# Route to the experts: residual's affine part moved to VectorE, tokens gathered as normalised values and modulated as columns

## The chip, the cores and the metric

One core of one Trainium2 chip runs the whole program. The metric is the device time of one execution in microseconds, lower is better. Three executions of the kernel before took 2433.91, 2436.0 and 2442.73 us; the median is 2436.0 us. The names used below: PE is TensorE, DVE is VectorE, ACT is ScalarE, POOL is GpSimd, SP is SyncE, whose queue issues the weight loads.

## The reference, cut to what matters

The program is two transformer blocks of two layers each on 256 tokens (and 256 context tokens) of width 1024, in float32. Only the two layers of the first block are touched. Each of them ends its mixer with a layer norm, a modulation, a router and a mixture of 32 experts:

```python
x = layer_norm(ALPHA * x + g1x * yx, ln1_g[l], ln1_b[l])     # layer 0 also for ctx, with its own g1c
ux = x * (1.0 + s2x) + sh2x                                  # layer 0: uc = ctx * (1.0 + s2c) + sh2c
y = hier_moe(tok, ...)                                       # top 2 of 32 experts, weights 1024x512, 1024x512, 512x1024
x = layer_norm(ALPHA * x + g2x * y, ln2_g[l], ln2_b[l])
```

With z the normalised row (before gain and bias), the experts' input is z * (g(1+s2)) + (b(1+s2) + sh2), and the residual is ALPHA * (z*g + b). In layer 0 there are 512 tokens (four tiles of 128: tiles 0 and 1 are x, tiles 2 and 3 are ctx, with different s2 and sh2); in layer 1 there are 256 (two tiles, one pair of s2 and sh2).

## The kernel before, in words

`out_ln` multiplies the mixer's output by its weight matrix, adds the residual, normalises each row and computes the router's logits. In layer 0 it does this in two passes, first for tiles 2 and 3, then for tiles 0 and 1. `normalise` leaves z in the residual's tile (`M.x`, called mx in the trace; in layer 1 it is xres). `modulate` then makes the experts' input: in layer 0 a product and a sum with two 128x1024 tiles A and B that hold gain and bias broadcast to all partitions (on POOL or DVE by the list `MODL`), and a split of the result into two float32r halves uh and ul (`split_T`: uh on ACT, ul on POOL), written with the columns permuted. In layer 1 only the split is done there; gain and bias enter later as columns. `route` ranks the tokens (a chain of small DVE instructions, L593 to L639, with three PE products between them). `modulate` for tiles 0 and 1 is queued behind the chain's mark (L574), and after it POOL multiplies each residual tile by ALPHA*g and adds ALPHA*b (L578 and L579, 128x1024 each).

`moe` runs the experts in units of two: 16 units in layer 0, 15 in layer 1, each with 12 weight tiles of 1 MB. The weights come on SP's queue into a ring of 11 tiles, in the order of the code; a tile is loaded again when PE has read it. `gather` collects the 128 token slots of a unit: DVE builds a one-hot matrix Pm (L735, L736: two instructions per token tile), PE multiplies uh and ul by it (L748), and ACT copies the result from PSUM to xT (L753; in layer 1 with scale and bias as columns, L759). Unit 0 is gathered alone, later units in pairs. `unit` multiplies xT by the gate and up weights (gu, L825), forms hh (L829 on ACT, L830 on DVE), transposes it (hT), multiplies by the down weights (ey, L851) and returns eight (four in layer 1) scatters: PE spreads the result back over the tokens (sc, L871 and L872), DVE scales it (gy, L875), POOL adds it to the residual (L876). From unit 1 on the order on PE is the order of the code; the scatters of the unit before and the gather of the next pair are put between the gu products by the lists `FILL` (the `work` callback). Before unit 0 the planner of the framework orders the instructions by readiness and by place in the code; `issue_after(m)` only keeps an instruction behind m on m's own engine. Between unit 0 and unit 1 stands a conditional block (`rest`, L967) that all engines pass. PSUM has four buffers for gathers, scatters and transposes together (`psB`).

Of the kernel before, what the change touches and what calls it, by code (L numbers as in the profile page):

```python
# [21 lines left out]
D = 1024  # L22
# [20 lines left out]
MODL = ((0, 1, 1, 0), (0, 0))  # L43
BOTH = (1, 0, 1)


# [86 lines left out]
class Kernel:  # L133
# [349 lines left out]
    def out_ln(self, M, W, lhs, L, ntt, xsrc):  # L483
        nc, I, ada = self.nc, self.I, self.ada[L]
        self.rate = RATE_O
        with self.pool("po") as p:
            g1 = [self.bcast(p, ada.dram[i, 2048:3072], D, f"g1_{i}") for i in range(ntt // 2)]
            lg = self.bcast(p, I["ln1_g"][L], D, "lng")
            lb = self.bcast(p, I["ln1_b"][L], D, "lnb")
            ns = ntt // 2  # L490
            WA, red = self.wa, self.red
            A, B = [], []
            for i in range(ns if L == 0 else 0):
                sh = self.bcast(p, ada.dram[i, 3072:4096], D, f"B{i}")
                sc = self.bcast(p, ada.dram[i, 4096:5120], D, f"A{i}")
                tmp = p.tile([128, D], F32, name="AB", tag="u", bufs=2)
                nc.gpsimd.tensor_scalar(sc, sc, 1.0, 1.0, op0=OP.mult, op1=OP.add)
                nc.gpsimd.tensor_mul(tmp, sc, lb)
                nc.gpsimd.tensor_add(sh, sh, tmp)
                nc.gpsimd.tensor_mul(sc, sc, lg)  # L500
                A.append(sc)
                B.append(sh)
            for v in (lg, lb):
                nc.gpsimd.tensor_scalar(v, v, ALPHA, 0.0, op0=OP.mult, op1=OP.add)
            if L == 0:
                for t in range(ntt):
                    nc.sync.dma_start(M.x[t], xsrc[t])
                xsrc = M.x
            else:
                M.cols = self.ucols  # L510
            z = M.x
            st = p.tile([128, ntt, 2, 6], F32, name="ln_st")
            norm = {}
            MOD = [(nc.gpsimd, nc.vector)[k] for k in MODL[0]]
            MOD1 = [(nc.gpsimd, nc.vector)[k] for k in MODL[1]]
# [6 lines left out]
            def modulate(t, eng):  # L522
                v8 = lambda a: a.rearrange("t (p j) -> t p j", j=8)
                jt = lambda a: a.rearrange("t j p -> t p j")
                if L == 0:
                    u = p.tile([128, 8, 128], F32, name="u", tag="u", bufs=2)
                    eng.tensor_mul(jt(u), v8(z[t]), v8(A[t // 2]))
                    eng.tensor_add(jt(u), jt(u), v8(B[t // 2]))
                    return self.split_T(M.uh[t], M.ul[t], u, nc.gpsimd)
                else:  # L530
                    return self.split_T(jt(M.uh[t]), jt(M.ul[t]), v8(z[t]), eng)

            def logits(c, tts):

                for t in tts:
                    pt = self.psB("zT")
                    for k in range(4):
# [12 lines left out]
                    nc.vector.bn_aggr(mv, st[:, t])  # L550
                    r = self.rsqrt(mv[:, 1:2], 1e-5, [128, 1], bufs=4)
                    norm[t] = (mv, r)
                    nc.vector.scalar_tensor_tensor(g, red[:, t // 2, 0], mv[:, 0:1], g, op0=OP.mult, op1=OP.add)
                    nc.vector.scalar_tensor_tensor(g, g, r, red[:, t // 2, 1], op0=OP.mult, op1=OP.add)

            for tts in (((2, 3), (0, 1)) if ntt > 2 else ((0, 1),)):
                def ev(c, tt, ps):
                    sl = slice(c * 512, c * 512 + 512)
                    gy = self.sb.tile([128, 512], F32, name="gy", tag="s512")
                    nc.vector.tensor_mul(gy, ps, g1[tt // 2][:, sl])  # L560
                    nc.vector.scalar_tensor_tensor(z[tt][:, sl], xsrc[tt][:, sl], ALPHA, gy,
                                                   op0=OP.mult, op1=OP.add)
                    nc.vector.bn_stats(st[:, tt, c], z[tt][:, sl])
                    if tt == tts[-1]:
                        logits(c, tts)
                self.lin_D(W, lhs, tts, ev, (0, 4), L == 1 and BOTH[0])
                for t in tts:
                    normalise(t)
                if tts[0] == 2:
                    for t in tts:  # L570
                        modulate(t, MOD[t])
# [148 lines left out]
    def gather(self, M, base, sl, places=(0,)):  # L720


        nc, n, p = self.nc, M.ntt, M.wp
        V = nc.vector
        stat = not isinstance(base, bass.AP)

# [15 lines left out]
        def part(c):  # L742
            pg = self.psB("xT")
            for a in range(per):
                j = per * c + a
                for t in ts:
                    for k, u in enumerate((M.uh[t], M.ul[t])):
                        nc.tensor.matmul(pg[:, a * w:a * w + w], u[:, j], Pm[:, t, :w],  # L748
                                         start=t == ts[0] and k == 0, stop=t == ts[-1] and k == 1)
            js = slice(per * c, per * c + per)  # L750
            for i in range(m):
                if M.cols is None:
                    xt = nc.scalar.activation(  # L753
                        xT[i][:, js], pg.rearrange("p (j m t) -> p m j t", m=m, t=128)[:, i], AF.Copy)
                    continue
# [6 lines left out]
        return xT, [lambda c=c: part(c) for c in range(2 * m)]  # L762

    def unit(self, M, base, experts, widths, room=2048, xT=None, work=None):

# [95 lines left out]
        yh = p.tile([128, 2, 512], F32R, name="yh", tag="yh", bufs=1)  # L861
        yl = p.tile([128, 2, 512], F32R, name="yl", tag="yl", bufs=1)
# [16 lines left out]
    def moe(self, M):  # L879
# [19 lines left out]
        for tag in ("yh", "yl"):  # L899
            M.wp.tile([128, 2, 512], F32R, name=tag, tag=tag, bufs=1)  # L900
        M.rows = None
        units = UNITS[L]

# [14 lines left out]
        def run(u, add, parts):  # L918
# [1123 lines left out]
```

## Time and profile before

| | before |
|---|---|
| median of three executions | 2436.0 us |
| profiled execution | 2441.86 us |
| its span | 2439.7 us |
| PE busy | 2218.6 us (91%) |
| DVE busy | 1254.7 us (51%) |
| ACT busy | 708.4 us (29%) |
| POOL busy | 537.6 us (22%) |
| mean granted TensorE clock (share of full) | 0.951 |
| HBM traffic | 266 GB/s over the span |
| a 512 KB weight load, from issue to landing | 10.2 us (median) |

The page gives busy time of each engine, the span in 40 slices, the DMA queues, the chain of work that ended last, and the costliest groups of instructions. A busy PE is not PE at its peak. In the timeline each row is a start time, a duration from the first start to the last end, the engine, the line, the operation, and how many instructions were merged; in brackets is how long the engine was idle before and who released it.

### The profile page before, as it was taken

What the parts mean: (1) busy time and instruction counts of PE and PEld (TensorE: products, weight loads), DVE (VectorE), ACT (ScalarE), POOL (GpSimd) and SP (SyncE); (2) the same over time, 40 slices, a digit from 0 to 9 for tenths busy, and PEclk for the clock granted to TensorE, in tenths of its full rate; (3) what the DMA queues carried; (4) which work ended last, traced back from release to release, by engine and by line L of the source; (5) the groups of instructions that cost most, each with busy time, mean ns of one, the idle gap of its engine ahead of it and who ended that gap; (6) DMA issues with size and microseconds to landing.
All of it is one profiled execution on the core that took longest, in us unless ns stands there. A gap on an engine that the chain in (4) does not pass through costs nothing. (4 is left out here: it accounts for less than half of the span.)

```text
span 2439.7 us, 35230 instructions
## 1 busy us (share of the span) xinstructions
PE 2218.6 (91%) x13185; PEld 1395.5 (57%) x13186; DVE 1254.7 (51%) x2724; ACT 708.4 (29%) x1179; POOL 537.6 (22%) x451
## 2 busy tenths in 40 slices
PE   7999995789999998899779999998899999858999
PEld 3786673444444443676633333332655998657997
DVE  3354767444444444757842322223774554666554
ACT  2215242111111111434421111111453543414442
POOL 2121334233333333300130211111201000561000
PEclk9999996699999999899979999999899999979999
DMA  8654365389999999443569999999554555737553
GB/s 301 249 193 156 134 213 223 129 342 408 408 409 409 409 408 373 155 173 132 191 240 384 409 408 408 409 409 380 190 191 172 191 176 186 261 107 274 186 179 120
DMA packets 209272, 652.36 MB, mean 267 GB/s; under 512 B 20668, under 2 KB 33965, under 8 KB 197568
## 3 DMA queue, kind: packets, MB, share of 16 engines
q1 hardware_dynamic: 201680, 632.24, 68.9%
q0 software_dynamic: 7408, 17.73, 2.2%
q8 instruction: 107, 1.75, 0.3%
q14 instruction: 77, 0.63, 0.1%
HBM read 648.65 MB, written 1.25 MB: 266 GB/s over the span
## 5 line engine op out<-in xcount | busy, mean ns | idle before, releaser
L825 PE MATMUL gu<-w,xT 128*32 128x512 f32 (+1 forms) x2880 | 493.0, 605 | 16.2 <-PEq L967 9.9
L201 DVE TENSOR_TENSOR wlo<-w,whi 128x1024 fp32r<-128x1024 f32 (+3 forms) x240 | 298.7, 1246 | 308.6 <-ACT whi L200 308.4
L200 ACT ACTIVATE whi<-w 128x1024 fp32r<-128x1024 f32 (+3 forms) x264 | 274.2, 1041 | 508.4 <-PE A L247 276.8
L825 PEld LDWEIGHTS gu<-w,xT 128*32 128x32 f32 (+1 forms) x2880 | 141.0, 121 | 315.5 <-issue 246.4
L1872 PE MATMUL A<-lhs_hi,wlo 128*128 128x256 f32 x864 | 246.5, 286 | 14.1 <-POOL wlo L201 13.6
L246 PE MATMUL A<-wlo,lhs_hi 128*128 128x512 f32 (+3 forms) x640 | 248.7, 389 | 9.5 <-DVE wlo L201 9.4
L245 PE MATMUL A<-whi,lhs_hi 128*128 128x512 f32 (+3 forms) x640 | 250.6, 396 | 5.9 <-ACT whi L200 2.8
L1870 PE MATMUL A<-lhs_hi,whi 128*128 128x256 f32 x864 | 247.8, 287 | 1.0 <-ACT whi L200 1.0
L1871 PE MATMUL A<-lhs_lo,whi 128*128 128x256 f32 x864 | 247.1, 286 | 0.0
L247 PE MATMUL A<-whi,lhs_lo 128*128 128x512 f32 (+3 forms) x640 | 246.6, 386 | 0.0
L876 POOL TENSOR_TENSOR mx<-mx,gy 128x512 f32<-128x512 f32 x124 | 161.5, 1331 | 355.0 <-DVE gy L875 354.9
L851 PE MATMUL ey<-w,hT 128*32 128x512 f32 (+1 forms) x1440 | 225.8, 595 | 9.5 <-ACT hT L838 9.5
L875 DVE TENSOR_TENSOR gy<-sc,g 128x512 f32<-128x512 f32 x188 | 121.5, 685 | 218.2 <-PE sc L872 215.8
L1872 PEld LDWEIGHTS A<-lhs_hi,wlo 128*128 128x128 f32 x864 | 167.8, 194 | 14.5 <-POOL wlo L201 13.8
L1870 PEld LDWEIGHTS A<-lhs_hi,whi 128*128 128x128 f32 x864 | 167.9, 195 | 7.1 <-issue 5.0
L1871 PEld LDWEIGHTS A<-lhs_lo,whi 128*128 128x128 f32 x864 | 168.0, 194 | 0.2 <-DVE lhs_lo L255 0.2
L876 POOL TENSOR_TENSOR xres<-xres,gy 128x512 f32<-128x512 f32 x58 | 74.3, 1293 | 380.0 <-DVE gy L875 379.1
L245 PEld LDWEIGHTS A<-whi,lhs_hi 128*128 128x128 f32 x640 | 123.1, 194 | 56.3 <-issue 17.7
L851 PEld LDWEIGHTS ey<-w,hT 128*32 128x32 f32 (+1 forms) x1440 | 68.3, 120 | 147.9 <-issue 115.6
L246 PEld LDWEIGHTS A<-wlo,lhs_hi 128*128 128x128 f32 x640 | 123.4, 193 | 39.6 <-DVE wlo L201 13.8
L748 PE MATMUL xT<-Pm,uh 128*128 128x256 f32 (+1 forms) x416 | 111.4, 303 | 29.4 <-DVE Pm L736 29.4
L247 PEld LDWEIGHTS A<-whi,lhs_lo 128*128 128x128 f32 x640 | 123.5, 193 | 24.2 <-issue 4.0
(586 smaller groups left out, 3264.8 us busy)
## 6 DMA issues: line engine op xcount, KB each, us to landing
w<-in_moe_w_gate_dram SPq DMA_DIRECT2D x248, 512.0 KB, 10.2
w<-in_moe_w_up_dram SPq DMA_DIRECT2D x248, 512.0 KB, 10.2
w<-in_moe_w_down_dram SPq DMA_DIRECT2D x248, 512.0 KB, 10.2
w<-in_ada_w_dram SPq DMA_DIRECT2D x88, 1024.0 KB, 6.7
w<-in_ffn_w_dram SPq DMA_DIRECT2D x64, 1024.0 KB, 5.1
w<-in_ab_w_in_dram SPq DMA_DIRECT2D x13, 1024.0 KB, 9.0
w<-in_c_w_qkv_dram SPq DMA_DIRECT2D x12, 1024.0 KB, 5.2
w<-in_ada_w_dram SPq DMA_DIRECT2D x16, 512.0 KB, 9.9
```

What stands on the lines that cost most here:

```text
L200: self.nc.scalar.activation(hv, w, AF.Copy)
L201: (eng or self.nc.vector).tensor_sub(lv, w, hv.bitcast(F32))
L245: nc.tensor.matmul(o, hi[:, kk, ts], wh[:, k], start=at + k == 0, stop=False)
L246: nc.tensor.matmul(o, hi[:, kk, ts], wl[:, k], start=False, stop=False)
L247: nc.tensor.matmul(o, lo[:, kk, ts], wh[:, k], start=False, stop=at + k == nk - 1)
L825: nc.tensor.matmul(pgu[m][a:b], xT[:, j, a:b], w[:, i, k], start=j == 0, stop=j == 7)
L851: nc.tensor.matmul(py[h][a:b], hT[:, j, a:b], w[:, i, k, h * 512:h * 512 + 512], start=j == 0, stop=j == 3)
L875: V.tensor_mul(gy, ps, M.g2[t // 2][:, h * 512:h * 512 + 512])
L876: eng.tensor_add(o, o, gy)
L1870: nc.tensor.matmul(o, wh[:, k, cs], hi[:, kk], start=kk == 0 and c % 2 == 0, stop=False)
L1871: nc.tensor.matmul(o, wh[:, k, cs], lo[:, kk], start=False, stop=False)
L1872: nc.tensor.matmul(o, wl[:, k, cs], hi[:, kk], start=False, stop=kk == 7 and c % 2 == 1)
```

## The change

In layer 0, `out_ln` no longer loads A and B as broadcast tiles. Six vectors are loaded as columns (128 partitions by 8) and combined by five small POOL instructions into scale columns for x and ctx, shift columns for ctx, and the difference of the two shifts. `modulate` becomes `parts`, in both layers only the split of z, with uh on ACT and ul on DVE. POOL's products and sums on the residual go. In `moe` two tiles that later hold the experts' results (yh and yl) first take g and b (loaded broadcast on POOL's queue, scaled by ALPHA on ACT), and `residual` does the products and sums on DVE, queued behind the Pm of units 1 and 2, from the `work` callback of unit 0. In layer 0, `gather` uses `part2`: the slots' share of x tokens is counted by a product of ones with Pm (of_x, plain float32, two products and a copy by ACT), ctx tokens and x tokens are gathered into separate halves of a PSUM buffer (a buffer holds half as many columns), and each 128x128 block is evicted by one ACT instruction and two DVE instructions instead of part of an ACT copy. `begin(1)`, which builds Pm for units 1 and 2, is called before unit 0 is written instead of after.

```diff
@@ out_ln
-            for i in range(ns if L == 0 else 0):
-                sh = self.bcast(p, ada.dram[i, 3072:4096], D, f"B{i}")
-                sc = self.bcast(p, ada.dram[i, 4096:5120], D, f"A{i}")
...
-            for v in (lg, lb):
-                nc.gpsimd.tensor_scalar(v, v, ALPHA, 0.0, op0=OP.mult, op1=OP.add)
+                cols = M.p.tile([128, 6, 8], F32, name="ucols0")
+                for k, v in enumerate((ada.dram[0, 4096:5120], ada.dram[1, 4096:5120], ada.dram[0, 3072:4096],
+                                       ada.dram[1, 3072:4096], I["ln1_g"][L], I["ln1_b"][L])):
+                    nc.gpsimd.dma_start(cols[:, k], v.rearrange("(p j) -> p j", j=8))
...
+            def parts(t):
                 v8 = lambda a: a.rearrange("t (p j) -> t p j", j=8)
                 jt = lambda a: a.rearrange("t j p -> t p j")
-                if L == 0:
-                    u = p.tile([128, 8, 128], F32, name="u", tag="u", bufs=2)
-                    eng.tensor_mul(jt(u), v8(z[t]), v8(A[t // 2]))
-                    eng.tensor_add(jt(u), jt(u), v8(B[t // 2]))
-                    return self.split_T(M.uh[t], M.ul[t], u, nc.gpsimd)
-                else:
-                    return self.split_T(jt(M.uh[t]), jt(M.ul[t]), v8(z[t]), eng)
+                self.split_T(jt(M.uh[t]), jt(M.ul[t]), v8(z[t]))
...
             for t in (0, 1):
                 with self.tc.issue_after(mark):
-                    last = modulate(t, MOD[t] if L == 0 else MOD1[t])
-            with self.tc.issue_after(last):
-                for t in norm:
-                    nc.gpsimd.tensor_mul(M.x[t], M.x[t], lg)
-                    nc.gpsimd.tensor_add(M.x[t], M.x[t], lb)
+                    parts(t)
@@ gather
+        def part2(c):
+            if c == 0:
+                pi = self.psB("of_x")
+                for t in range(2):
+                    nc.tensor.matmul(pi[:, :w], self.ones, Pm[:, t, :w].bitcast(F32), start=t == 0, stop=t == 1)
...
+                    nc.scalar.activation(f, pi[:, i * 128:i * 128 + 128], AF.Copy)
...
+            for j0 in range(per * c, per * c + per, per // 2):
+                pg = self.psB("xT")
+                for a in range(per // 2):
+                    for k, t in ((k, t) for k in (1, 0) for t in (2 * k, 2 * k + 1)):
...
+                        nc.scalar.activation(x, ps(0), AF.Identity, scale=A[:, 0, j:j + 1], bias=B[:, j:j + 1])
+                        V.scalar_tensor_tensor(x, ps(1), A[:, 1, j:j + 1], x, op0=OP.mult, op1=OP.add)
+                        xt = V.scalar_tensor_tensor(x, of_x[i], dB[:, j:j + 1], x, op0=OP.mult, op1=OP.add)
@@ moe
+        aff = [M.wp.tile([128, D], F32, name=f"aff_{tag}", tag=tag, bufs=1) for tag in ("yh", "yl")]
+        for a, v in zip(aff, (self.I["ln1_g"][L], self.I["ln1_b"][L])):
+            self.bcast(None, v, D, "", to=a)
+            nc.scalar.activation(a, a, AF.Copy, scale=ALPHA)
+        def residual(t):
+            for h in range(2):
+                sl = slice(h * 512, h * 512 + 512)
+                nc.vector.tensor_mul(M.x[t][:, sl], M.x[t][:, sl], aff[0][:, sl])
+                nc.vector.tensor_add(M.x[t][:, sl], M.x[t][:, sl], aff[1][:, sl])
...
             def work(c):
+                if u == 0 and c < 2:
+                    for t in range(c * n // 2, c * n // 2 + n // 2):
+                        with tc.issue_after(M.marks[0]):
+                            residual(t)
...
+        next_two = begin(1)
         add, _ = run(0, deque(), deque())
         while add:
             add.popleft()()
-        for f in begin(1):
+        for f in next_two:
             f()
```

## Rows read from the trace of the kernel before

**Rows 1.** Windows of layer 0: width, busy per engine (instructions), granted clock, DMA share, GB/s

```profile
433.00:452.00 19.00, 10.22 (x46) 9.90 (x46) 11.24 (x13) 0.60 (x1) 10.93 (x7) 0.50 0.18 55
600.00:700.00 100.00, 100.00 (x827) 44.55 (x827) 43.66 (x94) 13.38 (x29) 32.45 (x25) 1.00 1.03 408
```

**Rows 2.** Timeline of POOL behind the ranking, layer 0: first of four residual rows

```profile
424.27 4.68 POOL L578 TENSOR_TENSOR mx<-mx,lng 128x1024 f32<-128x1024 f32 x2
```

**Rows 3.** Groups of DVE between 424 and 444 us: count, busy us, mean ns, idle

```profile
L735 DVE TENSOR_SCALAR Pm<-iota,su 128x128 fp32r<-128x128 f32 x4 | 9.2, 2340 | 0.1
L736 DVE SCALAR_TENSOR_TENSOR Pm<-iota,su,Pm 128x128 fp32r<-128x128 f32 x4 | 7.5, 1911 | 0.0
L638 DVE TENSOR_TENSOR r_ov<-r_fc,r_R 128x128 f32<-128x128 f32 x1 | 2.5, 2467 | 0.0
L732 DVE TENSOR_SCALAR su<-r_sl 128x8 f32<-128x8 f32 x1 | 1.9, 1869 | 0.0
```

**Rows 4.** Timeline of DVE in the ranking chain and in unit 0, layer 0

```profile
404.91 2.33 DVE L608 TENSOR_SCALAR r_gc<-r_gc 128x16 f32<-128x16 f32 x1
...
407.27 3.15 DVE L611 TENSOR_TENSOR r_Em<-lg,r_gc 128x32 f32<-128x32 f32 x4
...
413.86 0.29 DVE L615 SCALAR_TENSOR_TENSOR r_Em<-r_ec,r_Em 128x128 f32<-128x128 f32 x1
...
416.92 1.93 DVE L527 TENSOR_TENSOR u<-mx,A 128x1024 f32<-128x1024 f32 x1
...
463.07 0.60 DVE L736 SCALAR_TENSOR_TENSOR Pm<-iota,su,Pm 128x128 fp32r<-128x128 f32 x2
```

**Rows 5.** Timeline of layer 0's two passes: first evictions, last logits, one wait

```profile
340.03 1.28 DVE L560 TENSOR_TENSOR gy<-A,g 128x512 f32<-128x512 f32 x2
...
359.37 1.00 PE L543 MATMUL lg<-WA,zT 128*128 128x36 f32 x8
...
370.46 0.67 DVE L560 TENSOR_TENSOR gy<-A,g 128x512 f32<-128x512 f32 x1
...
374.35 0.80 PE L246 MATMUL A<-wlo,lhs_hi 128*128 128x512 f32 x1 [5.17 <-DVE wlo L201]
...
400.64 1.08 PE L543 MATMUL lg<-WA,zT 128*128 128x36 f32 x8
```

**Rows 6.** Window of the second pass, columns as in the first group

```profile
371.00:389.00 18.00, 13.53 (x43) 11.18 (x44) 12.06 (x11) 4.96 (x6) 8.30 (x3) 0.54 0.17 58
```

**Rows 7.** Timeline of unit 0 and its end, layer 0

```profile
472.03 0.35 DVE L736 SCALAR_TENSOR_TENSOR Pm<-iota,su,Pm 128x128 fp32r<-128x128 f32 x1
479.02 0.75 PE L152 MATMUL hT<-ident,hh 128*128 128x128 f32 x4 [0.85 <-DVE hh L830]
...
489.85 10.03 POOL L876 TENSOR_TENSOR mx<-mx,gy 128x512 f32<-128x512 f32 x8 [45.91 <-DVE gy L875]
...
504.94 15.97 PE L825 MATMUL gu<-w,xT 128*32 128x512 f32 x128 [4.96 <-PEq L967]
```

**Rows 8.** Instructions on tile mx: count, ns minimum/median/maximum, first and last start

```profile
L876 DVE TENSOR_TENSOR mx<-mx,gy x4: 665/674/810, 960.0 to 965.5; 128x512 f32<-128x512 f32 x4
```

**Rows 9.** Timeline of later units of layer 0

```profile
649.33 3.62 PE L825 MATMUL gu<-w,xT 128*32 128x512 f32 x32
...
671.91 0.69 DVE L830 TENSOR_TENSOR hh<-gu,hh 128x512 f32<-128x512 f32 x1 [2.20 <-PE gu L825]
...
948.97 7.71 PE L851 MATMUL ey<-w,hT 128*64 128x512 f32 x32
```

**Rows 10.** Timeline of the ranking chain in layer 1

```profile
1216.47 3.67 ACT L254 ACTIVATE uh<-xres 128x1024 fp32r<-128x1024 f32 x2
...
1218.70 2.71 DVE L600 TENSOR_TENSOR r_fc<-r_fc,r_ff 128x64 f32<-128x64 f32 x1
...
1224.26 4.53 DVE L622 TENSOR_TENSOR r_M<-r_M 128x32 f32<-128x32 f32 x2
...
1231.13 2.29 DVE L634 TENSOR_TENSOR r_R<-r_R,bonus 128x64 f32<-128x64 f32 x1
```

More of the change, by code (lines that the diff above doesn't have):

```diff
@@ L42 @@
 LNE = 1
-MODL = ((0, 1, 1, 0), (0, 0))
 BOTH = (1, 0, 1)
@@ L487, in out_ln @@
             g1 = [self.bcast(p, ada.dram[i, 2048:3072], D, f"g1_{i}") for i in range(ntt // 2)]
-            lg = self.bcast(p, I["ln1_g"][L], D, "lng")
-            lb = self.bcast(p, I["ln1_b"][L], D, "lnb")
-            ns = ntt // 2
             WA, red = self.wa, self.red
-            A, B = [], []
-            for i in range(ns if L == 0 else 0):
-                sh = self.bcast(p, ada.dram[i, 3072:4096], D, f"B{i}")
-                sc = self.bcast(p, ada.dram[i, 4096:5120], D, f"A{i}")
-                tmp = p.tile([128, D], F32, name="AB", tag="u", bufs=2)
+            if L == 0:
+                cols = M.p.tile([128, 6, 8], F32, name="ucols0")
+                for k, v in enumerate((ada.dram[0, 4096:5120], ada.dram[1, 4096:5120], ada.dram[0, 3072:4096],
+                                       ada.dram[1, 3072:4096], I["ln1_g"][L], I["ln1_b"][L])):
+                    nc.gpsimd.dma_start(cols[:, k], v.rearrange("(p j) -> p j", j=8))
+                sc, sh, g, h = cols[:, 0:2], cols[:, 2:4], cols[:, 4:5], cols[:, 5:6]
+                tmp = p.tile([128, 2, 8], F32, name="ucols_t")
+                two = lambda a: a.to_broadcast([128, 2, 8])
                 nc.gpsimd.tensor_scalar(sc, sc, 1.0, 1.0, op0=OP.mult, op1=OP.add)
-                nc.gpsimd.tensor_mul(tmp, sc, lb)
+                nc.gpsimd.tensor_mul(tmp, sc, two(h))
                 nc.gpsimd.tensor_add(sh, sh, tmp)
-                nc.gpsimd.tensor_mul(sc, sc, lg)
-                A.append(sc)
-                B.append(sh)
-            for v in (lg, lb):
-                nc.gpsimd.tensor_scalar(v, v, ALPHA, 0.0, op0=OP.mult, op1=OP.add)
-            if L == 0:
+                nc.gpsimd.tensor_mul(sc, sc, two(g))
+                nc.gpsimd.tensor_tensor(cols[:, 2], cols[:, 2], cols[:, 3], op=OP.subtract)
+                M.cols = cols
                 for t in range(ntt):
@@ L513, in out_ln @@
             norm = {}
-            MOD = [(nc.gpsimd, nc.vector)[k] for k in MODL[0]]
-            MOD1 = [(nc.gpsimd, nc.vector)[k] for k in MODL[1]]
             def normalise(t):
@@ L570, in out_ln @@
                     for t in tts:
-                        modulate(t, MOD[t])
+                        parts(t)
             mark = self.route(M, p)
@@ L574, in out_ln @@
                 with self.tc.issue_after(mark):
-                    last = modulate(t, MOD[t] if L == 0 else MOD1[t])
-            with self.tc.issue_after(last):
-                for t in norm:
-                    nc.gpsimd.tensor_mul(M.x[t], M.x[t], lg)
-                    nc.gpsimd.tensor_add(M.x[t], M.x[t], lb)
+                    parts(t)
     def route(self, M, q):
@@ L720, in gather @@
     def gather(self, M, base, sl, places=(0,)):
-        nc, n, p = self.nc, M.ntt, M.wp
+        nc, n, L, p = self.nc, M.ntt, M.L, M.wp
         V = nc.vector
@@ L749, in part @@
                                          start=t == ts[0] and k == 0, stop=t == ts[-1] and k == 1)
-            js = slice(per * c, per * c + per)
             for i in range(m):
[L752 to L755, printed above, removed]
                 for a in range(per):
@@ L761, in part @@
             M.marks[1] = xt.ins
-        return xT, [lambda c=c: part(c) for c in range(2 * m)]
+        of_x = []
+        def part2(c):
[3 more added lines that the diff above has]
+                    nc.tensor.matmul(pi[:, :w], self.ones, Pm[:, t, :w].bitcast(F32), start=t == 0, stop=t == 1)
+                for i in range(m):
+                    if m == 1:
+                        f = self.sb.tile([128, 512], F32, name="of_x", tag="s512")[:, :128]
+                    else:
+                        f = M.p.tile([128, n, 32], F32, name="of_x", tag=("r_ec", "r_fc")[i])
+                        f = f.rearrange("p n e -> p (n e)")
+                    nc.scalar.activation(f, pi[:, i * 128:i * 128 + 128], AF.Copy)
+                    of_x.append(f)
+            A, B, dB = M.cols[:, 0:2], M.cols[:, 3], M.cols[:, 2]
+            for j0 in range(per * c, per * c + per, per // 2):
+                pg = self.psB("xT")
+                for a in range(per // 2):
+                    for k, t in ((k, t) for k in (1, 0) for t in (2 * k, 2 * k + 1)):
+                        o = (2 * a + k) * w
+                        for i, u in enumerate((M.uh[t], M.ul[t])):
+                            nc.tensor.matmul(pg[:, o:o + w], u[:, j0 + a], Pm[:, t, :w],
+                                             start=t == 2 * k and i == 0, stop=t == 2 * k + 1 and i == 1)
+                for a in range(per // 2):
+                    j = j0 + a
+                    for i in range(m):
+                        ps = lambda k: pg[:, (2 * a + k) * w + i * 128:(2 * a + k) * w + i * 128 + 128]
+                        x = xT[i][:, j]
+                        nc.scalar.activation(x, ps(0), AF.Identity, scale=A[:, 0, j:j + 1], bias=B[:, j:j + 1])
+                        V.scalar_tensor_tensor(x, ps(1), A[:, 1, j:j + 1], x, op0=OP.mult, op1=OP.add)
+                        xt = V.scalar_tensor_tensor(x, of_x[i], dB[:, j:j + 1], x, op0=OP.mult, op1=OP.add)
+            M.marks[1] = xt.ins
+        return xT, [lambda c=c: (part if L else part2)(c) for c in range(2 * m)]
     def unit(self, M, base, experts, widths, room=2048, xT=None, work=None):
@@ L859, in unit @@
                     nc.tensor.matmul(py[h][a:b], hT[:, j, a:b], w[:, i, 0], start=j == 0, stop=j == 3)
-        yh = p.tile([128, 2, 512], F32R, name="yh", tag="yh", bufs=1)
-        yl = p.tile([128, 2, 512], F32R, name="yl", tag="yl", bufs=1)
+        yh, yl = (p.tile([128, D], F32R, name=k, tag=k, bufs=1).rearrange("t (h d) -> t h d", h=2)
+                  for k in ("yh", "yl"))
         for h in range(2):
@@ L898, in moe @@
         M.chain = [*CHAIN, None]
-        for tag in ("yh", "yl"):
-            M.wp.tile([128, 2, 512], F32R, name=tag, tag=tag, bufs=1)
+        aff = [M.wp.tile([128, D], F32, name=f"aff_{tag}", tag=tag, bufs=1) for tag in ("yh", "yl")]
[7 more added lines that the diff above has]
+                nc.vector.tensor_add(M.x[t][:, sl], M.x[t][:, sl], aff[1][:, sl])
         M.rows = None
```

2 lines of the change are left out of this document (removed).

## The prediction

> **What bounds the kernel now.** I read the windows of the two expert stages first, then the timelines of POOL and DVE ahead of unit 0, then the waits of PE. The chain of waits could not be used for layer 0: it reaches back only to the conditional block of layer 1.
>
> In the middle of layer 0's experts PE is busy all the time and the weights flow at 408 GB/s [rows 1]; both are full there, so this stretch gives nothing back and can only get longer. Ahead of it is a hole: from 433 to 452 us the queues move 55 GB/s, PE is half idle at half clock, and POOL and DVE work [rows 1]. The weight ring is full and waits for PE to release a tile, and PE waits for Pm. So each microsecond by which unit 0 starts earlier should move all that follows, as long as the ring is full at that moment, which it is.
>
> What DVE does in this hole is the point. Eight Pm instructions take 16.7 us, 2340 and 1911 ns each [rows 3]; the same L736 takes 0.30 us in unit 0 [rows 4]. Beside the slow ones POOL runs four pairs of residual instructions without a gap, 2.34 us each, about 18.7 us in all (one pair shown) [rows 2]. The slow DVE instructions have the length of a POOL instruction, whatever their own size: a product of 128x128 took 2467 ns, an operation on eight columns 1869 ns [rows 3]. So DVE waits for POOL, instruction by instruction, and PE waits for DVE.
>
> **The change part by part.**
>
> *The ranking chain of layer 0.* Without POOL's products each DVE instruction should take its own time. Pm: 16.7 us becomes eight times 0.30 [rows 3, 4], 14.3 us saved. The three short instructions of the chain that were caught once (first at 404.91, last L638) took 2.1 to 2.5 us where the like of them takes 0.29 [rows 3, 4]: 6.2 us. The four at 407.27 took 3.15 us for at most 0.29 each [rows 4]: 2.0 us. L732 took 1.87 for at most as much [rows 3]: 1.6 us. Together 24.1 us. In exchange DVE gets the two ul halves of tiles 0 and 1 in the chain, but it had tile 1's product and sum there at 1.93 us each [rows 4], so this is even. uh of tiles 0 and 1 (1.84 us each with permuted columns [rows 10]) lies on ACT while DVE ranks.
>
> *The second pass of layer 0.* The first pass went from its first eviction at 340.03 to its last logits at 360.4, 20.3 us; the second from 370.46 to 401.7, 31.3 us, with a wait of 5.17 us for DVE in it [rows 5], after which the granted clock was 0.54, that is 1.2 GHz for most of it [rows 6]. In that wait DVE sat in tile 2's product and sum beside POOL's. Now ACT has 3.7 us of uh [rows 10] and DVE some 3.9 us of ul more than in the first pass, and no POOL. The bounds are 5 us (the wait alone) and 11 us (the first pass's length); I take 9, since the wait and the low clock behind it should both go.
>
> *Unit 0's start.* of_x adds two float32 products. The gu products (two instructions each in the counts) issue 32 in 3.62 us, four side by side [rows 9], so one instruction of 512 columns takes 0.45 us and two products of 128 columns, at half clock, about 0.9. The rest of the evictions overlaps with gu, which starts with the first columns. I add 1 us.
>
> *Residual on DVE.* 16 instructions of 0.67 us [rows 8], 10.7 us, queued behind the Pm of units 1 and 2. That Pm ended at 472.4, and hh, which PE waits for, came at 478.2 [rows 7]: 5.8 us of room. As residual stands ahead of hh in the code, I expect all of it in front of hh. So hh is late by 10.7 less 5.8, about 5 us. It may be 3 us more, since the slot computation is now queued behind the last evictions, which are on DVE (some ten instructions of 0.3 us); or nothing, if the planner puts hh first. Between 0 and 8 I take 4, nearest to the plain difference.
>
> *The gather between units 0 and 1.* It was evicted by ACT. Now DVE does two instructions for each of 16 blocks, 32 times 0.30 [rows 4], 9.7 us, and in the same stretch POOL adds unit 0's scatters, eight in 10.03 us, until 499.9 [rows 7]. PE needs PSUM buffers back before its last columns, and only then passes the conditional block (4.96 us before, and again after) [rows 7]. The bounds are 1 us (of_x alone) and 8 us (all evictions in line behind POOL). I take 3.5.
>
> A rule of the Trainium skill bears here. The page "SBUF — State Buffer", section "Who interferes with whom", says that a DVE instruction with two SBUF inputs is blocked by a GpSimd instruction that reads SBUF for the whole of it, and one with a single SBUF input outside the two-port modes is not. The trace agrees as far as it goes, since the two-input product above took 2467 ns. By this rule the second of the new DVE instructions (of_x and x both in SBUF) meets POOL's adds and the first (one input in PSUM) does not, which is the third rival below.
>
> *Units 1 to 15 of layer 0.* The six pairs and the single unit that are gathered here pay for of_x: two products of 256 columns are 0.9 us by the same rows [rows 9], 5.9 us in all, on a PE that had no gap [rows 1]. Then hh: in a unit with a gather DVE was idle for 2.2 us before it [rows 9], and 16 more DVE instructions (4.8 us) now come before hh; so hh comes up to 2.6 us late. PE has a quarter of the gather to do in between, which covers part; between 0 and 2.6 I take 1.5 us a pair, 9 us for six. At the end PE had caught up with the weights (its last ey, 32 instructions two side by side, took 7.71 us where the pace above gives 7.2) [rows 9], so it has some 2 us to give away. Sum 12 to 13; I take 12, with bounds of 2 (DVE hidden) and 24 (3 us a pair).
>
> *Layer 1.* The same relief in the chain: six instructions between 1218.70 and 1233.4 took 13.6 us (first, one pair and last shown) [rows 10] where at most 0.29 each would do, 11.9 us saved. But the two ul halves, POOL's before, are now on DVE behind the mark, 3.9 us, of which some 1 us was waited for PE there anyway: 2.9 us back. Net 9, bounds 6 and 12. Its gather is untouched, and its residual (eight instructions, 5.4 us) fits in front of hh. The weights bound layer 1's later units, but their stream restarts with PE's release there too.
>
> *The rest at nothing.* The six column loads and five small POOL instructions lie under PE's passes; without cover they would cost about one load's latency, 10 us by the weight loads in the table, but nothing reads them until the first eviction. The two broadcast loads of g and b and their scaling (about 2 us of ACT) have the gather's first products as cover; if late they hold ACT's evictions back, at most 2 us.
>
> **Sum.** -24.1 - 9 + 1 + 4 + 3.5 = -24.6 to unit 1's start; +12 in layer 0's later units, -12.6; -9 in layer 1; -21.6 us in all. The profiled execution took 2441.9 us (span 2439.7), 5.9 above the median, so it gives 2420.3 there and 2414.4 against the median. I predict 2414.
>
> **Rivals.**
>
> *The relief is whole and DVE's new work hides* (0.22). hh is not late, and later units pay for of_x alone less their slack: -33.1 + 1 + 1 + 4 - 9 = -36, 2400 us. For it: DVE was 44% busy in the middle [rows 1]. Against it: the work falls into the units' narrow places.
>
> *Layer 0's gain is eaten in layer 0* (0.10). PE falls back to half clock behind a late hh, as it did in the second pass [rows 6], and later units lose 3 us a pair: -33.1 + 1 + 13 + 8 + 20 = +9, and with layer 1's -9 nothing is left: 2430 to 2436 us. For it: both PE and the queues were full [rows 1]. Against it: it takes all the upper bounds at once.
>
> *Evictions locked by POOL* (0.06), the slower side. 16 second instructions a pair each wait for one POOL add of 1.25 us [rows 7] and POOL for them: 20 us on top of 9.7, where a unit takes 30 us and the gather begins in its middle. It decides from 7 us of lost PE time a pair: seven pairs then lose 49 us against 42 saved. At 10 us a pair it is 2436 - 42 + 70 = 2464. For it: the slow Pm shows what one such wait costs [rows 3]. Against it: between two bursts of scatters POOL is idle, 32 of 100 us busy [rows 1].
>
> *The slow DVE instructions are not POOL's doing* (0.04). Then only the order changes, and the time stays at 2436 or rises by the 12 us. Against it: in length they match POOL's instructions and go back to 0.30 when POOL stops.
>
> **Chances.** The forecast has 0.58. Its own range follows from the bounds, 2400 to 2427; the range for 8 in 10 takes in most of the second and third case: 2394 to 2432. 0.5% is 12 us, about what a measurement of this kernel can tell from no change. Faster than 2424 is the forecast but for a tail of 0.04, and the whole-relief case: 0.76. Within it are that tail, the eaten gain and most of the last case: 0.17. Slower are the locked evictions and the rest: 0.07.
>
> **What would show it.** Pm of unit 0 at about 0.3 us each, with the last ending some 34 us earlier than 443.2; no wait of 5 us for DVE in the second pass and full clock there; hT of unit 0 waiting some 4 us for hh; the pairs of later units about 2 us longer on PE; in layer 1 unit 1's first gu about 9 us earlier relative to its logits. The prediction is wrong if Pm stays slow, if PE in later units waits for PSUM or hh by more than 3 us a pair, or if unit 0's earlier start finds no weights.

## The result, and the profile after

The changed kernel takes 2408.3 us (median of four executions, 2401.5 to 2411.1) against 2437.2 us for the kernel before on the same chip: ratio 0.9884, 95% interval 0.9866 to 0.9901. The forecast was 2414 with a range of 2394 to 2432. The profiled execution took 2407.1 us with a span of 2405.4 us, so 34.3 us less span than the one of before, of which some 5 us are there because the profiled execution of before, 2441.9 us, lay above its median.

The table cuts the span at ten instructions of the timelines and gives each stretch its length in us, for the kernel before, the changed kernel, and the experiments that are told below (names as there). "gu 1" is the first gate product of unit 1, "sc" the first scatter of unit 0.

| stretch | before | after | late | noscale | first best | poolres | resalone | actonly |
|---|---|---|---|---|---|---|---|---|
| start to last logits, layer 0 | 401.7 | 393.5 | 393.5 | 393.0 | 392.1 | 397.0 | 397.5 | 390.0 |
| logits to end of last Pm | 41.5 | 16.7 | 16.7 | 16.7 | 16.7 | 24.9 | 25.3 | 16.7 |
| Pm to first gu of unit 0 | 13.4 | 16.8 | 16.6 | 14.5 | 14.5 | 14.5 | 13.4 | 15.1 |
| gu to hT | 22.4 | 26.1 | 20.8 | 26.6 | 20.1 | 21.2 | 22.9 | 21.9 |
| hT to sc | 8.5 | 11.5 | 8.5 | 11.7 | 8.5 | 8.5 | 8.5 | 8.5 |
| sc to gu 1 | 17.4 | 21.7 | 21.5 | 21.6 | 21.6 | 21.5 | 17.2 | 17.8 |
| gu 1 to end of layer 0's last ey | 451.7 | 451.2 | 450.9 | 451.5 | 450.6 | 451.2 | 450.0 | 449.4 |
| ey to last logits, layer 1 | 255.8 | 253.4 | 254.3 | 253.7 | 254.1 | 255.6 | 254.0 | 253.8 |
| logits to first gather product, layer 1 | 23.4 | 13.4 | 13.5 | 13.4 | 13.4 | 21.4 | 16.6 | 13.4 |
| that to end of layer 1's last ey | 457.5 | 456.8 | 457.9 | 455.9 | 456.9 | 455.7 | 460.7 | 456.0 |
| ey to the end | 746.3 | 744.2 | 741.7 | 742.3 | 745.3 | 742.1 | 744.6 | 741.4 |

Where the hole of [rows 1] was, this is the window of the changed kernel (columns as there):

```profile
405.00:425.00 20.00, 13.01 (x60) 12.82 (x60) 7.50 (x26) 4.24 (x8) 3.27 (x6) 0.50 0.84 336
```

The gather now runs while the weights are still being loaded. VectorE's timeline from the ranking chain to the last Pm answers to [rows 3, 4]:

```profile
397.12 0.49 DVE L595 TENSOR_TENSOR r_Em<-lg,r_gc 128x32 f32<-128x32 f32 x4
...
402.33 1.92 DVE L254 TENSOR_TENSOR ul<-mx,uh 128x1024 fp32r<-128x1024 f32 x1
...
408.04 0.17 DVE L716 TENSOR_SCALAR su<-r_sl 128x8 f32<-128x8 f32 x1
408.24 0.48 DVE L719 TENSOR_SCALAR Pm<-iota,su 128x128 fp32r<-128x128 f32 x2
...
409.56 0.61 DVE L720 SCALAR_TENSOR_TENSOR Pm<-iota,su,Pm 128x128 fp32r<-128x128 f32 x2
```

Each instruction has its own length: four Em take 0.49 us instead of 3.15, su 0.17 instead of 1.87, a Pm instruction about 0.3 instead of 1.9 to 2.3. The last Pm ends at 410.2 us instead of 443.2. PE's timeline shows what of these 33 us is left by unit 1 (it answers to [rows 5, 7]):

```profile
392.40 1.08 PE L531 MATMUL lg<-WA,zT 128*128 128x36 f32 x8 [0.75 <-ACT zT L528]
...
426.95 4.91 PE L839 MATMUL gu<-w,xT 128*64 128x512 f32 x14
...
453.08 1.13 PE L151 MATMUL hT<-ident,hh 128*128 128x128 f32 x4 [6.70 <-DVE hh L844]
454.89 9.72 PE L865 MATMUL ey<-w,hT 128*64 128x512 f32 x32 [0.69 <-ACT hT L852]
464.62 1.21 PE L885 MATMUL sc<-yh,PT 128*128 128x512 f32 x4
...
486.33 4.50 PE L839 MATMUL gu<-w,xT 128*32 128x512 f32 x20 [6.03 <-DVEq L995]
```

Three stretches are longer than before. PE waits 6.70 us for hh, which stands behind all of residual on VectorE:

```profile
442.64 0.68 DVE L922 TENSOR_TENSOR mx<-mx,aff_yh 128x512 f32<-128x512 f32 x1
...
451.14 1.28 DVE L923 TENSOR_TENSOR mx<-mx,aff_yl 128x512 f32<-128x512 f32 x2
452.34 0.68 DVE L844 TENSOR_TENSOR hh<-gu,hh 128x512 f32<-128x512 f32 x1
```

What follows begins at half clock (ey 9.72 us instead of 7.09, hT 1.13 instead of 0.75; the granted clock was 0.50 from 453 to 459 us and 1.00 from 461). The gather of unit 0 takes 3.4 us more, and ScalarE's timeline says why:

```profile
411.22 0.28 ACT L756 ACTIVATE of_x<-of_x 128x128 f32<-128x128 f32 x1 [7.60 <-PE of_x L749]
419.03 1.06 ACT L917 ACTIVATE aff_yh<-aff_yh 128x1024 f32<-128x1024 f32 x1 [7.53 <-DMA aff_yh<-in_ln_g_dram]
419.99 0.44 ACT L772 ACTIVATE xT<-xT,ucols 128x128 f32<-128x128 f32 x1
421.51 1.06 ACT L917 ACTIVATE aff_yl<-aff_yl 128x1024 f32<-128x1024 f32 x1 [1.08 <-DMA aff_yl<-in_ln_b_dram]
```

The two scalings stand in ScalarE's order ahead of the first and second eviction, and their loads, issued on GpSimd's queue at 408 us, land at 419 and 421.5. And from sc to gu 1 VectorE's two instructions a block come last to the conditional block (the bracket at 486.33 names VectorE; before it named PE):

```profile
472.00 0.69 DVE L889 TENSOR_TENSOR gy<-sc,g 128x512 f32<-128x512 f32 x1 [0.56 <-POOL mx L890]
...
473.48 0.70 DVE L773 SCALAR_TENSOR_TENSOR xT<-xT,ucols 128x128 f32<-128x128 f32 x2
474.09 1.88 DVE L774 SCALAR_TENSOR_TENSOR xT<-of_x,ucols,xT 128x128 f32<-128x128 f32 x2
...
482.65 0.34 DVE L773 SCALAR_TENSOR_TENSOR xT<-xT,ucols 128x128 f32<-128x128 f32 x1
```

In layer 1 the chain answers to [rows 10]. No instruction is stretched, and the first gather product comes 13.4 us after the last logits instead of 23.4:

```profile
1198.09 1.91 DVE L254 TENSOR_TENSOR ul<-xres,uh 128x1024 fp32r<-128x1024 f32 x1
1199.90 0.20 DVE L617 TENSOR_SCALAR r_R<-r_R 128x64 f32<-128x64 f32 x1
...
1203.94 0.61 DVE L720 SCALAR_TENSOR_TENSOR Pm<-iota,su,Pm 128x128 fp32r<-128x128 f32 x2
```

### The profile page after: what moved, and what is told of

The parts are those of the page before. It is cut to its first block, busy times and chain, and to the rows that moved or that the text cites. A ratio compares the mean times of both kernels' runs of the same rounds, so it can differ in the third digit from the quotient of the medians.

```text
span 2405.4 us, 35653 instructions
## 1 busy us (share of the span) xinstructions
PE 2216.5 (92%) x13221; PEld 1393.6 (58%) x13222; DVE 1293.7 (54%) x3006; ACT 750.0 (31%) x1267; POOL 460.5 (19%) x424
## 5 line engine op out<-in xcount | busy, mean ns | idle before, releaser
L839 PE MATMUL gu<-w,xT 128*32 128x512 f32 (+1 forms) x2880 | 485.0, 603 | 16.2 <-DVEq L995 6.0
L1900 PE MATMUL A<-lhs_hi,wlo 128*128 128x256 f32 x864 | 246.5, 286 | 14.1 <-POOL wlo L200 13.5
L1900 PEld LDWEIGHTS A<-lhs_hi,wlo 128*128 128x128 f32 x864 | 167.8, 194 | 14.5 <-POOL wlo L200 13.7
L244 PEld LDWEIGHTS A<-whi,lhs_hi 128*128 128x128 f32 x640 | 122.0, 192 | 58.7 <-issue 18.5
L246 PEld LDWEIGHTS A<-whi,lhs_lo 128*128 128x128 f32 x640 | 121.9, 191 | 24.8 <-issue 4.0
L879 DVE SCALAR_TENSOR_TENSOR yl<-ey,wsl,yh 128x512 fp32r<-128x512 f32 x62 | 46.5, 750 | 137.0 <-ACT yh L878 135.7
## 6 DMA issues: line engine op xcount, KB each, us to landing
w<-in_moe_w_gate_dram SPq DMA_DIRECT2D x248, 512.0 KB, 10.2
w<-in_moe_w_up_dram SPq DMA_DIRECT2D x248, 512.0 KB, 10.2
w<-in_moe_w_down_dram SPq DMA_DIRECT2D x248, 512.0 KB, 10.2
```

What stands on the lines that cost most here:

```text
L244: nc.tensor.matmul(o, hi[:, kk, ts], wh[:, k], start=at + k == 0, stop=False)
L246: nc.tensor.matmul(o, lo[:, kk, ts], wh[:, k], start=False, stop=at + k == nk - 1)
L839: nc.tensor.matmul(pgu[m][a:b], xT[:, j, a:b], w[:, i, k], start=j == 0, stop=j == 7)
L1900: nc.tensor.matmul(o, wl[:, k, cs], hi[:, kk], start=False, stop=kk == 7 and c % 2 == 1)
```

## The experiments

All times are against the kernel before on the same chip: 2439.7 us (median of 7) for the first four, 2435.2 (median of 9) for the others.

**poolres: residual back on GpSimd, the rest of the change kept.**

```diff
+            with self.tc.issue_after(last):
+                for t in norm:
+                    nc.gpsimd.tensor_mul(M.x[t], M.x[t], lg)
+                    nc.gpsimd.tensor_add(M.x[t], M.x[t], lb)
...
-                            residual(t)
```

> The changed kernel with residual put back on GpSimd behind the last split, as it was before, with its loads and scalings; the gather with columns stays. Theory A (the slow VectorE instructions were GpSimd's doing, residual's above all): the eight Pm instructions of layer 0 take about 2 us each again and the last ends 14 to 16 us later than in the changed kernel, in layer 1 about 8 us later; against it hT's wait of 6.70 us, the half clock behind it (2.6) and the late loads (2.4) go: about 2420 us. Rival B (they were slow for another reason, such as the permuted or modulated columns): Pm stays at 0.3 us, and only the costs beside unit 0 go, 2397 us.

Measured: 2418.2 us, ratio 0.992 (0.9894 to 0.9946). The time is as theory A has it, the place is not (in layer 0 the last Pm ends 8.2 us later behind the logits than in the changed kernel, not 14 to 16): GpSimd took the residual of tiles 2 and 3 in the second pass (368 to 381 us), where PE then waited 2.6 us, so only two tiles were left for the chain. The timeline of VectorE and, under it, that of GpSimd show the mechanism:

```profile
409.92 2.32 DVE L626 TENSOR_TENSOR r_R<-r_R,r_R 128x128 f32<-128x128 f32 x1
412.92 2.09 DVE L629 TENSOR_TENSOR r_ov<-r_fc,r_R 128x128 f32<-128x128 f32 x1
415.04 0.29 DVE L630 TENSOR_REDUCE r_sl<-r_ov 128x4 f32<-128x128 f32 x1
415.36 1.87 DVE L723 TENSOR_SCALAR su<-r_sl 128x8 f32<-128x8 f32 x1
417.33 3.06 DVE L726 TENSOR_SCALAR Pm<-iota,su 128x128 fp32r<-128x128 f32 x2
420.32 0.60 DVE L727 SCALAR_TENSOR_TENSOR Pm<-iota,su,Pm 128x128 fp32r<-128x128 f32 x2
```

```profile
407.91 4.17 POOL L570 TENSOR_TENSOR mx<-mx,lng 128x1024 f32<-128x1024 f32 x1 [11.95 <-DVE r_R L624]
...
417.76 2.35 POOL L571 TENSOR_TENSOR mx<-mx,lnb 128x1024 f32<-128x1024 f32 x1
```

VectorE has slow instructions from 408 to 420 us, while GpSimd works, and the Pm instruction that starts when GpSimd has ended (420.1) takes 0.3 us again. Rival B falls. Not every instruction is held up: the TENSOR_REDUCE at 415.04 takes 0.29 us during a GpSimd product (414.82 to 417.20), as another did at 424.48 in the kernel before, during the pair of [rows 2]. So the prediction's "instruction by instruction" is too wide: in these rows it holds for instructions with two tiles from SBUF and for TENSOR_SCALAR, not for reductions. In layer 1 the chain is 21.4 us long again. With residual off VectorE, hT does not wait (gu to hT 21.2 us, hT to sc 8.5), and with the scalings gone gu starts 2.3 us sooner behind Pm.

**resalone: the kernel before with residual alone moved**, its loads and scalings with it. `begin(1)` stays behind unit 0.

```diff
-                    nc.gpsimd.tensor_mul(M.x[t], M.x[t], lg)
-                    nc.gpsimd.tensor_add(M.x[t], M.x[t], lb)
...
+                            residual(t)
```

> The kernel before with residual alone moved to VectorE beside the first unit, as in the changed kernel; tokens are still modulated ahead of the gather (tiles 0 and 3 on GpSimd) and gathered as they were, without of_x. Theory A (residual on GpSimd slows Pm, the modulation of tile 0 on GpSimd slows the chain ahead of it): Pm at 0.3 us, its last end 14 to 16 us earlier after the last logits, but the short instructions ahead of it stay at 2 to 2.5 us; the second pass keeps its wait of 5 us; unit 0 pays for residual in front of hh as in the changed kernel (about 9 us); layer 1 gains some 5 to 6. In all 10 to 14 us faster than before, about 2424 us. Rival B (the gain belongs to the columns): no faster than before, 2437 or more, as hh is late and nothing is won.

Measured: 2411.1 us, ratio 0.9883 (0.9858 to 0.9907), as much as the whole change. The chain is as theory A expected (logits to Pm 16.2 us shorter, the instructions beside GpSimd's modulation still slow), but unit 0 pays nothing for residual:

```profile
403.06 3.15 DVE L605 TENSOR_TENSOR r_Em<-lg,r_gc 128x32 f32<-128x32 f32 x4
...
422.20 0.61 DVE L730 SCALAR_TENSOR_TENSOR Pm<-iota,su,Pm 128x128 fp32r<-128x128 f32 x2
430.30 1.90 DVE L903 TENSOR_TENSOR mx<-mx,aff_yh 128x512 f32<-128x512 f32 x3 [6.39 <-ACT aff_yh L898]
...
439.60 0.69 DVE L904 TENSOR_TENSOR mx<-mx,aff_yl 128x512 f32<-128x512 f32 x1
...
458.42 0.69 DVE L824 TENSOR_TENSOR hh<-gu,hh 128x512 f32<-128x512 f32 x1 [5.69 <-PE gu L819]
```

Here ScalarE evicts the gather, VectorE is free, and residual runs between 430 and 440, ahead of the slot computation; hh waits for PE and not the other way round. In the changed kernel residual begins at 442.6, and hh stands behind it. Two things differ between them, and no run takes them apart: VectorE evicts unit 0's gather there, and residual is queued behind another mark. The mark (`M.marks[0]` in the code) is the last Pm built so far; with `begin(1)` ahead of unit 0 this is the Pm of units 1 and 2, which ends at 440.3, and in resalone it is still the Pm of unit 0, which ends at 422.8. So residual was not placed "as in the changed kernel", as the expectation says. The gains of the two parts do not add: alone they save 28.7 us (residual) and 21.5 us (the columns, residual on GpSimd), together 28.9. In layer 0 the columns bring Pm 12.6 us further forward than residual alone does (410.2 against 422.8), and by gu 1 the changed kernel is 1.4 us behind it (486.3 against 484.9). By the table the 14 us go to unit 0's gather (3.4), hh (3.2), the half clock behind it (3.0) and the evictions ahead of unit 1 (4.5). Rival B falls too. Our estimate was too small because it also charged hh, and because the second pass ended 4.2 us earlier, for a reason told at the end.

**late: only tile 0's residual ahead of hh.**

```diff
-                if u == 0 and c < 2:
-                    for t in range(c * n // 2, c * n // 2 + n // 2):
+                if u == 0 and c in (1, 3):
+                    for t in ((0,) if c == 1 else range(1, n)):
```

> The changed kernel, but only tile 0's residual is issued ahead of hh of unit 0 (and of layer 1's unit 0); the other tiles follow behind hh. Theory A (hh is late only because residual stands in front of it on VectorE, and the half clock behind it is a consequence): hT of unit 0 waits under 1 us for hh instead of 6.70, its ey takes 7.1 us instead of 9.72, and unit 1's first gu comes 8 to 9 us earlier; as the weights bound what follows, the whole of it arrives at the end: about 2399 us against 2408. Rival B (the later start of yl, with residual now between hh and it, takes the place): yl waits for VectorE by 3 to 6 us and the end gains at most 3 us. Rival C (unit 1's start is set by the scatters, the evictions and the conditional block, whatever unit 0 does): unit 0 ends earlier, unit 1's first gu does not, 2408.

Measured: 2397.9 us, ratio 0.983 (0.9806 to 0.9855). As theory A has it:

```profile
447.56 0.75 PE L151 MATMUL hT<-ident,hh 128*128 128x128 f32 x4 [0.85 <-DVE hh L844]
448.99 7.09 PE L865 MATMUL ey<-w,hT 128*64 128x512 f32 x32 [0.69 <-ACT hT L852]
...
477.60 12.85 PE L839 MATMUL gu<-w,xT 128*32 128x512 f32 x100 [5.84 <-DVEq L995]
```

No wait for hh beyond 0.85 us, full clock (1.00 from 446 to 456 us), unit 1 8.7 us earlier, and layer 0's end 9.0 us earlier. VectorE has ended the moved residual at 454.2 and then waits 1.8 us for yh, so rival B has no ground; rival C falls with gu 1.

**noscale: ALPHA inside residual, no scaling on ScalarE.**

```diff
-            nc.scalar.activation(a, a, AF.Copy, scale=ALPHA)
...
+                nc.vector.scalar_tensor_tensor(x, x, ALPHA, aff[0][:, sl], op0=OP.mult, op1=OP.mult)
+                nc.vector.scalar_tensor_tensor(x, aff[1][:, sl], ALPHA, x, op0=OP.mult, op1=OP.add)
```

> The changed kernel without ScalarE's scaling of the two broadcast rows by ALPHA: residual takes ALPHA in its own two instructions. Theory A (the scalings, queued in order on ScalarE and waiting for loads that land at 419 and 421 us, hold back unit 0's first evictions): the first eviction comes at about 412 instead of 419.99, no wait of 2.03 us of PE for it, and unit 0's first gu comes 3 to 4 us earlier after the last Pm (16.8 us after its end now); hT's wait for hh then stays about the same, as all of VectorE's work moves with it; 2405 us. Rival B (the gather at half clock is bound by PE, not by the evictions): first eviction earlier, gu's start within 0.5 us of now, 2408.

Measured: 2403.0 us, ratio 0.9854 (0.9829 to 0.9879); too close to the changed kernel's to tell the two times apart, so the trace decides.

```profile
410.76 0.28 ACT L756 ACTIVATE of_x<-of_x 128x128 f32<-128x128 f32 x1 [7.60 <-PE of_x L749]
414.12 0.46 ACT L772 ACTIVATE xT<-xT,ucols 128x128 f32<-128x128 f32 x1 [3.08 <-PE xT L765]
...
417.49 0.46 ACT L772 ACTIVATE xT<-xT,ucols 128x128 f32<-128x128 f32 x1 [2.02 <-PE xT L765]
```

The first eviction comes at 414.1, when PE has the first columns, instead of 420.0 (5.9 us sooner, not 8), and gu starts 14.5 us behind the last Pm instead of 16.8. Theory A, with 2.3 us instead of 3 to 4: the rest of the gather is paced by PE, at a granted clock of 0.50 from 410 to 424 us, as the waits for PE of 2 us between the later evictions show. hT waits the same 6.70 us.

**first best: both, with layer 1's residual left as it was.**

> Residual of tiles 1 to 3 behind hh in layer 0 alone (layer 1 as in the changed kernel) together with ALPHA inside residual, so without ScalarE's two scalings. If the two costs are separate they add: hT waits under 1 us, the first gu of unit 0 comes 16.8 - 2.4 = 14.4 us after the last Pm, unit 1's first gu 11 us earlier than in the changed kernel, and about 12 us off the time, 2396 us. If they share their time (the gather of unit 0 then waits for something else): 2398 to 2400, no better than the first of the two alone.

Measured: 2395.1 us, ratio 0.9835 (0.9819 to 0.9852), beside the changed kernel run anew on the same chip at 2405.6 us, ratio 0.989 (0.987 to 0.991). The two intervals do not overlap, so this version beats both kernels. Its stretches are those of late and noscale together (14.5, 20.1, 8.5): the costs are separate. From the last Pm to gu 1 it takes 64.7 us instead of 76.2, 11.5 less.

The changed kernel run anew was this:

> The changed kernel again, unaltered, as the standard for the others on the same chip: 2408 us, first gu of unit 1 of layer 0 some 18 to 19 us earlier than in the kernel before.

Its first gu of unit 1 came at 487.1 us, 17.8 earlier than before and 0.8 later than in the first profile; its time was 2405.6.

**ofx4: each of_x of units 1 to 15 computed four times.**

```diff
-                for t in range(2):
+                for t in [0, 1] * (4 if stat and base else 1):
```

> The changed kernel, in which PE computes each of_x of units 1 to 15 of layer 0 four times over (the last stays): 20.1 us more work for PE (three times 6.7 us). Theory A (the stream of the weights sets the pace of these units and PE follows it with slack that its rows don't show as waits): from unit 1's first gu to the last ey of layer 0 451.2 us become 453 to 464, less than half to two thirds of the added work; of_x itself then cost nothing. Rival B (PE sets the pace, and of_x was made up for elsewhere): 471 us, 20 us on the time.

Measured: 2425.4 us (one execution), and from gu 1 to the last ey 468.2 us, 17.0 more than in the changed kernel. By their groups the added products are worth 15.6 us in the pairs (21.7 against 6.1; back to back they overlap, so the 20.1 of the expectation was too high) and at most 1.8 in the single unit, so they cost about all that they take. Read alone that is rival B. But the DMA rows of the same stretch (340 us in the middle of layer 0), for the kernel before, the changed kernel and this one, tell why the first 6.7 us were free:

```profile
560.00:900.00 340.00, 339.42 (x2146) 149.62 (x2139) 154.37 (x299) 42.32 (x86) 116.37 (x90) 1.00 1.03 409
```

```profile
541.00:881.00 340.00, 340.00 (x2174) 151.00 (x2166) 200.49 (x473) 64.11 (x137) 114.80 (x88) 1.00 1.03 408
```

```profile
541.00:881.00 340.00, 340.00 (x2190) 157.67 (x2189) 193.81 (x467) 64.98 (x140) 109.01 (x84) 1.00 1.02 398
```

PE is "busy" throughout in all three, but before and after the weights flow at their full 408 to 409 GB/s, and here at 398. SyncE's queue shows the same from the other side: in these 340 us it waited for PE to free a weight tile 4.2 us before (sum of four rows), 18.6 after and 46.0 here. Two of these rows for each kernel (us in total, times, longest):

```profile
SPq L814 <- PE ey L851: 1.5, 4, 0.6
...
SPq L814 <- PE gu L825: 1.0, 3, 0.4
```

```profile
SPq L828 <- PE ey L865: 12.8, 16, 4.0
SPq L828 <- PE gu L839: 2.4, 8, 0.6
```

```profile
SPq L828 <- PE ey L865: 33.3, 23, 5.2
SPq L828 <- PE gu L839: 9.7, 16, 1.8
```

PE's own rows show the slack as well, between gu 1 and the end of layer 0 (first the kernel before, then the changed one; busy us, mean ns):

```profile
L825 PE MATMUL gu<-w,xT 128*64 128x512 f32 x512 | 121.7, 598 | 0.6 <-DMA w<-in_moe_w_gate_dram 0.2
L839 PE MATMUL gu<-w,xT 128*64 128x512 f32 x512 | 115.7, 596 | 0.0
```

The same 512 instructions cover 6.0 us less in the changed kernel, and the ey of these units 2.0 us less (56.7 instead of 58.7), while of_x adds 6.7; in ofx4 this gu stays at 115.7. So before the change the stream set the pace, and PE was some 7 us faster over the whole of layer 0 (an estimate, from these rows and from the 6.7 us that cost no time); of_x used this up, and what is added now PE pays in full. Neither theory as written was right: A in the kind of bound, B in the price of more.

**actonly: late, with ScalarE alone evicting layer 0's gathers.** VectorE's two instructions a block are left out, that is the ctx tokens and the difference of the shifts (called the second image's in the expectation).

```diff
-                        V.scalar_tensor_tensor(x, ps(1), A[:, 1, j:j + 1], x, op0=OP.mult, op1=OP.add)
-                        xt = V.scalar_tensor_tensor(x, of_x[i], dB[:, j:j + 1], x, op0=OP.mult, op1=OP.add)
```

> The kernel with residual behind hh (the first of these experiments), in which ScalarE alone evicts layer 0's gathers: VectorE's two instructions a block are left out, and with them the second image's tokens and shift. Theory A (VectorE's evictions make the stretch from unit 0's scatters to unit 1's first gu 4.3 us longer, since VectorE comes last to the conditional block; in the later units they are hidden): that stretch takes 17.4 us instead of 21.5, unit 0's gather 1 to 3 us less, and the 451 us behind it stay within 2 us: 2392 us. Rival B (the conditional block or GpSimd's adds set that stretch): 21 to 22 us as now. Rival C (the evictions also cost the later units time): those take 445 us or less.

Measured: 2386.1 us (one execution). From sc to gu 1 17.8 us instead of 21.5, and the conditional block is entered last by PE again:

```profile
452.17 1.21 PE L883 MATMUL sc<-yh,PT 128*128 128x512 f32 x4
...
469.96 10.36 PE L837 MATMUL gu<-w,xT 128*32 128x512 f32 x80 [4.07 <-PEq L993]
```

Theory A: VectorE's evictions cost 3.7 us there, 1.5 in unit 0's gather, and in all later units together no more than 1.5 (449.4 against 450.9). Rivals B and C fall. The 11.8 us between late and this run are not all theirs: 3.4 us lie ahead of layer 0's last logits, where the two kernels are alike, and 1.9 in layer 1's units; from gu to hT it takes 1.1 us more.

## Why the prediction was right, and where it was not

*The ranking chain (-24.1).* Measured -24.8. The cause is shown by poolres and resalone, in both directions.

*The second pass (-9).* Measured -8.2, and the wait of 5.17 us is gone. How much of it belongs to that wait alone is open (last section).

*Unit 0's start (+1).* Measured +3.4. The step that failed is the one put "at nothing", that the loads of g and b have "the gather's first products as cover". They were late, as the text allowed for ("at most 2 us"), and noscale gives their price, 2.3 us.

*hh late (+4).* Measured +3.8 on gu to hT, but another 3.0 from hT to sc, as PE fell to half clock behind the wait of 6.70 us. The forecast priced the wait and left the clock to the rival "eaten in layer 0"; late shows that both go with one cause: with three quarters of residual behind hh, unit 1 starts 8.7 us earlier.

*The gather between units 0 and 1 (+3.5).* Measured +4.3, of which actonly takes back 3.7. The larger part is the count of VectorE's instructions, which follow each other almost without a gap from 472.6 to 483.0 us. GpSimd's adds stretch the second instruction while they run (until 477.1), to 1.88 us for two at the most; over its fifteen instances that is 1.7 us, and no run takes the two apart. Here the Trainium skill's rule (page "SBUF — State Buffer", section "Who interferes with whom"), that an instruction with two SBUF inputs contends with a GpSimd instruction that reads SBUF, agrees with the trace: the instruction with two SBUF inputs took 459 ns on average between 466 and 484 us, the one with a PSUM input 338, and in the later units both take 346. Of the slow Pm of before, L735 is a TENSOR_SCALAR with one tile from SBUF, beside a column of scalars, and took 2340 ns [rows 3]. The same section counts tensor_scalar among the operations that can enter a two-port mode and then contend with GpSimd; whether this one ran in such a mode no run here shows.

*Sum to unit 1.* -18.6 instead of -24.6.

*Layer 0's later units (+12).* Measured -0.5: this is the term that was mis-sized. It was argued from "a PE that had no gap" [rows 1]. A row of PE lasts until its modelled end, so PE looks full when it follows the weights; ofx4 shows that it had some 7 us to spare and that of_x just fitted. The forecast gave PE "some 2 us to give away", from one ey. The other half, hh late by 1.5 us a pair, did not happen: PE's waits for hh in these units are 1.7 us in all, before and after. The bounds reached from 2 to 24, so even the lower end was too high. Rival 1 ("the whole relief, hidden DVE") was nearer on this point, with +4, and wrong on hh of unit 0.

*Layer 1 (-9).* Measured -10.0 from the logits to the gather. Another 2.4 us come ahead of it and were not foreseen: the stretch before layer 1's logits takes 255.6 and 255.8 us in the two kernels in which GpSimd scales the broadcast g and b, and 253.4 to 254.3 in the eight other profiles. Why was not tried.

*In all.* The terms up to unit 1 were 6 us too good, layer 0's later units 12.5 us too bad, and the rest gained some 6 more than forecast, 2.1 of it behind layer 1, where the ten profiles of this study spread over 741.4 to 746.3 and nothing can be told. That makes 12.7 us more in the profiled pair (34.3 against 21.6); between the medians, 28.9 us apart, it is some 7. That the forecast held is in part luck: two errors of opposite sign met. The rival "evictions locked by POOL" did not come, and "not POOL's doing" is refuted by poolres.

## What to carry to other kernels

When an engine is relieved of work, price the two parts of a change also in each other's presence: residual cost PE almost nothing in resalone, and 8.7 us by the start of unit 1 in the changed kernel, where VectorE also evicts and residual is queued behind a later Pm (which of the two does it is not shown). An instruction that only prepares something for later, and waits for a load, must not stand ahead of urgent ones in an engine's order. A PE that is busy in every slice is not shown to be the bound: look at whether the weights flow at their full rate and at how long the load queue waits for PE, since added work is free until that wait grows.

## What was not expected of the hardware

The half clock behind a wait does not last the same time in equal work. The kernel before and resalone both have the wait of 5.2 us in the second pass, with the same instructions around it. The granted clock was 0.50 from 373 to 389 us before, and from 374 to 380 us in resalone. From 385 to 395 us it was 0.77 before and 1.00 in resalone:

```profile
385.00:395.00 10.00, 10.00 (x38) 8.29 (x38) 3.20 (x4) 1.06 (x1) 0.00 (x0) 0.77 0.12 33
```

```profile
385.00:395.00 10.00, 10.00 (x56) 6.79 (x55) 5.24 (x10) 1.66 (x2) 0.00 (x0) 1.00 0.47 136
```

The logits ended 4.2 us apart, so up to that much of the second pass's 8.2 us may be this and not the change. Even the seven profiles whose code is the same up to these logits spread from 390.0 to 393.8 us. What decides how long it lasts was not tried. And the broadcast loads of g and b took 10.9 and 13.0 us from issue to landing while the queues were filling the weight ring; a 512 KB weight load took 10.2 (median).
